# One transpose for two triangles of a query block's weights, with held constants, a halved last accumulator and a later half reload

## The chip, the cores and the metric

The kernel runs on one core of one Trainium2 chip. Its metric is the device time of one execution in microseconds (us). Three runs of the kernel before took 1166.5, 1167.22 and 1168.82 us; the median is 1167.22. One more execution was profiled; it took 1166.51 us, of which 1164.5 lie between its first and its last instruction (its span).

The engines are named as in the profile: PE multiplies matrices, PEld is its loading of weights, DVE, ACT and POOL work elementwise, SP issues the transfers (DMAs).

## What is computed

A trunk of two layers over 1024 tokens of width 1024, in float32: a gated linear attention layer (layer A), then a layer with dilated sliding-window attention (layer B), each closed by an output projection, a residual and a layer norm. The change touches above all the attention of layer B. Each of its 8 heads attends in three groups of windows, and the groups' results are weighted by a softmax over their log-sums:

```python
SWA_GROUPS = ((128, 1), (512, 4), (2048, 16))      # window, dilation
...
    kcat, vcat = with_prev(kb), with_prev(vb)      # the block before, then the block itself
    scores = jnp.einsum('brnqgpe,brnkge->brngpqk', qb, kcat)
    qi = jnp.arange(blk)[:, None]
    kj = jnp.arange(2 * blk)[None, :]
    rel = blk + qi - kj
    band = (rel >= 0) & (rel <= w_sub)
...
    p = jnp.exp(scores - m)
    den = jnp.sum(p, axis=-1)
    o = jnp.einsum('brngpqk,brnkge->brnqgpe', p, vcat) / jnp.moveaxis(den, -1, 3)[..., None]
```

In the first two groups `w_sub` is 128, a block's length. Query i of a block therefore sees key j of its own block where j <= i, and key j of the block before where j >= i. The two triangles share a 128x128 square but for the diagonal, which belongs to both.

## The kernel before

The program is not issued in the order in which it is written. Every instruction is recorded as an `Op`; `Sched.order` then walks through time with a table of costs, gives each instruction the engine that is free first (`S.vp`: DVE or POOL; `S.va`: DVE or ACT), and among those that could start at a time takes the one with the smallest `prio`, which is its place in the program plus a shift (`S.later`). The result is a fixed order on each engine. So a changed cost or one more instruction anywhere can change which instruction stands beside which elsewhere. Where PE waits for data of one stage, the order places matmuls of a projection (tile `acc`) between: they are the filler that keeps PE occupied.

Large matmuls use `float32r` operands split in a high and a low part (`split_hi` on ACT, `split_lo` on DVE or POOL), three matmuls for each product (`mm3`). Attention's own matmuls are float32, and the trace shows each as two records; a transpose (a matmul with `ident`) is one record.

The program's parts, in order:

- The start (in `layer_a`): x arrives transposed, in eight tiles `xf` of 128x1024 with weights `wf`, is split into `xh`, `xl`, and multiplied into eight accumulators `pro`. The first tile is loaded in two halves, the others whole. The small constants (`b2c`, `ident`, `ngc`, `lngc`, `lnbc`) are loaded among them.
- Layer A, head by head (gates, `levels`, `state_prep`, projections, `chunks`, `finish`), its results kept in DRAM as `ogA`. Within the last head `reload_og` brings the six tiles of heads 0 to 2 back (`ogf`) and splits them into `ogh`, `ogl`, the first half of the tokens and then the second.
- `out_ln` for both halves, then layer B: keys and values; for each unit u (a head) `q_proj`, `scores` and `attend`.
- `scores(u)` writes the weights P: for groups 1 and 0 in tiles of two query blocks, each block 128 or 256 keys wide (one block without a block before it, or two). DVE adds the mask and takes the maximum, ACT takes the exponential.
- `attend(u)`: P is scaled by `cw`; group 2 is transposed into `diag` and multiplied with V; then `turn` transposes the 128x128 pieces of P that groups 1 and 0 need, up to four into one PSUM tile `ms`, and ACT or DVE copies them to SBUF as `PT`. Group 1 takes 3 pieces for each of 4 residues, group 0 15 pieces in four calls. `pv` multiplies them with V into two banks `po`. In group 0 a piece of a block and the next block's piece for the same keys go through as one matmul 256 wide.
- `out_ln(1, ...)` for the first half of the tokens, and `out_ln_rows(j, ...)` for j = 4 to 7, the blocks of the second half: two accumulators of 512 columns, `bn_stats` of each, `bn_aggr`, ACT's two steps for 1/sqrt, two passes on DVE, and two stores. The last of these ends the program.

Of the kernel before, what the change touches and what calls it, by code (L numbers as in the profile page):

```python
# [134 lines left out]
class Op:  # L135
    __slots__ = ("engs", "calls", "reads", "writes", "prio", "deps", "nuse", "cost", "t0", "t1", "eng", "func",
                 "first", "succ", "left", "seq", "port")


class Sched:  # L140
# [4 lines left out]
    def __init__(self, tc, lat, pad):  # L145
# [5 lines left out]
        self.extra = 0.0  # L151
# [9 lines left out]
    def record(self, engs, meth, args, kw):  # L161
# [20 lines left out]
        if g is None:  # L182
            o = Op()
            o.engs, o.calls, o.reads, o.writes, o.cost = engs, [], [], [], [0.0] * len(engs)
            o.func, o.prio, o.seq = func, len(self.ops) + self.shift, len(self.ops)
            o.port = [shares_port(e, meth, outs, ins) for e in engs]
            self.ops.append(o)
        else:
            o = g
            if not o.calls:  # L190
                o.engs, o.cost, o.func = engs, [0.0] * len(engs), func
                o.port = [False] * len(engs)
                o.prio, o.seq = len(self.ops) + self.shift, len(self.ops)
                self.ops.append(o)
# [6 lines left out]
    def group(self):  # L201
        return _Group(self)

# [45 lines left out]
    def order(self):  # L249
# [62 lines left out]
        while n_done < len(ops):  # L312
            best = None
            for e in self.ENG:
                cand = None
                for o in ready[e]:
                    if o.t0 is not None:
                        continue
                    r = 0.0
# [24 lines left out]
            if o.func is not None and e == "ACT":  # L344
                new = act_set(o.func, cur_set)
                if new != cur_set:
                    c += 1.3
# [133 lines left out]

class _Landing:
# [93 lines left out]
def trunk(tc, xT, wP, wA, wA12, wAv3, w2, b2, ng, wO, wK, wV0, wV12, wB, wOB, lng, lnb,  # L576
          ident_d, lmask_d, cos_d, sin_d, bmask_d, rmask_d, lnr_d, out):
# [93 lines left out]
    ngc = const.tile([128, NK], F32, name="ngc")  # L671
    lngc = const.tile([128, 2, NK], F32, name="lngc")
    lnbc = const.tile([128, 2, NK], F32, name="lnbc")
# [5 lines left out]
    def load_consts():  # L679
        S.sync.dma_start(ident, ident_d)  # L680
        S.vector.memset(onesr.bitcast(F32), 1.0)
        S.sync.dma_start(ngc, ng)
        S.sync.dma_start(lngc, lng)
        S.sync.dma_start(lnbc, lnb)
# [18 lines left out]
    def layer_a(t2, t1, after):  # L703
        lmask = t2.tile([128, NLEV - 2, 32], U8, name="lmask")
        smask = t2.tile([128, 512], F32, name="smask")
        b2c = t2.tile([128, GH], F32, name="b2c")
# [59 lines left out]
        for kt in range(NK):  # L766
# [14 lines left out]
            for r in (hs(0), hs(1)) if kt == 0 else (slice(0, T),):  # L781
# [9 lines left out]
        S.sync.dma_start(lmf, lmask_d)  # L791
        S.vector.tensor_copy(lmask, lmf)
        S.sync.dma_start(b2c, b2)
        w2f = xtile(F32, "w2f", (96, 512))
        S.sync.dma_start(w2f, w2)
# [217 lines left out]
        for h in range(GH):  # L1013
# [3 lines left out]
            for f in ('qg', 'qVg', 'qg', 'vge')[h]:  # L1017
                {"g": lambda: proj_g(h), "q": lambda: proj_qk(h + 1), "V": proj_v12, "v": lambda: proj_v(3), "e": after}[f]()
            for g in range(2):
                chunks(h, g)  # L1020
                finish(h, g)

# [65 lines left out]
    def out_ln_rows(j, wo, gam, bet):  # L1088
        xr = [small("res", tag, 2) for tag in ("t1", "t2")]
        rt = []  # L1090
        st = hp.tile([128, 2, 6], F32, name="lnst", bufs=2)
        for f in range(2):
            fs = hs(f)
            with S.later(-EVAC):
                S.sync.dma_start(xr[f], x1t[j - 4][:, fs])
            acc = bank(1, 2 * j + f)
            for kt in range(NK):
                (oh, ol), (wh, wl) = ogs[kt], wo[kt]
                with S.group():
                    S.tensor.matmul(acc, blk(oh, j), wh[:, fs], start=(kt == 0), stop=False)  # L1100
                    S.tensor.matmul(acc, blk(oh, j), wl[:, fs], start=False, stop=False)
# [522 lines left out]
```

## Time and profile before

| what | us |
|---|---|
| median of three runs | 1167.22 |
| the profiled execution | 1166.51 |
| its span, first to last instruction | 1164.5 |
| PE busy | 1154.5 |
| DVE busy | 766.6 |
| ACT busy | 483.0 |
| POOL busy | 166.0 |

The granted clock of PE was 0.998 of full speed over the span. A row of the chain of waits gives a start, a length and the engine and tile whose work filled it ("x9" counts records); it follows from the last instruction back through whatever released each step. All instructions of the program's body carry the line of the one call that issues them (L441 before, L446 after), so groups are told apart by tiles.

### The profile page before, as it was taken

The page shows a single profiled execution, that of the slowest core. Times are in us where ns is not written, and L with a number is a line of the kernel's source. Part 1 is how long each engine was busy: PE and PEld are TensorE (multiplying, and loading weights), DVE is VectorE, ACT ScalarE, POOL GpSimd, SP SyncE. Part 2 cuts the span into 40 slices and gives each one's busy share as a digit, 9 for nine tenths or more (in the row PEclk, how much of TensorE's full clock was granted, in tenths as well). Part 3 has the DMA queues.
Part 4 walks back from the last instruction along what each step waited for, and adds up shares of the span by engine and source line. Part 5 has one row for each costly group of instructions (what it writes and reads, how often), then busy time and mean ns, then how long its engine had stood idle before and what let it go on. Part 6 is the DMA issues. An engine that isn't in the chain of part 4 may idle for free.

```text
span 1164.5 us, 19529 instructions
## 1 busy us (share of the span) xinstructions
PE 1154.5 (99%) x7748; PEld 980.5 (84%) x7748; DVE 766.6 (66%) x1494; ACT 483.0 (41%) x1020; POOL 166.0 (14%) x101
## 2 busy tenths in 40 slices
PE   9999999999999999999999999999999999999997
PEld 8888888889987888888888888888888888888885
DVE  6294952685967697764366657574757676646578
ACT  5355541555463345311214433435333543545242
POOL 1001000202222131311021202020202111103000
PEclk9999999999999999999999999999999999999999
DMA  7111122111143463543611111111142011034545
GB/s 259 64 39 37 66 81 90 39 56 55 56 169 127 145 216 128 188 138 115 193 55 38 37 38 56 38 55 38 38 164 38 20 38 34 24 93 145 183 142 181
DMA packets 93227, 108.18 MB, mean 93 GB/s; under 512 B 44016, under 2 KB 62064, under 8 KB 93136
## 3 DMA queue, kind: packets, MB, share of 16 engines
q1 hardware_dynamic: 93136, 106.94, 29.2%
q8 instruction: 61, 1.00, 0.4%
q14 instruction: 30, 0.25, 0.1%
HBM read 85.74 MB, written 21.17 MB: 92 GB/s over the span
## 4 chain that ended last, share of the span: by engine, by line
PE 98%; DVE 0%; DMA 0%; ACT 0%; SPq 0%; issue 0%; DVEq 0%; ACTq 0%
PE acc L441 65%; PE po L441 10%; PE lv L441 9%; PE vac L441 8%; PE ms L441 5%; PE pro L441 2%; DMA xf<-in_xT 0%; DVE rt L441 0%; SPq L441 0%; DVE diag L441 0%; ACT xh L441 0%; DVE lnst L441 0%; DVE ogl L441 0%; DVE oT L441 0%; DVEq L1617 0%
## 5 line engine op out<-in xcount | busy, mean ns | idle before, releaser
L441 PE MATMUL acc<-x1h,wh 128*128 128x512 f32 x608 | 250.5, 412 | 0.0
L441 PE MATMUL acc<-x1h,wl 128*128 128x512 f32 x608 | 237.5, 391 | 0.0
L441 PE MATMUL acc<-x1l,wh 128*128 128x512 f32 x608 | 237.0, 390 | 0.0
L441 ACT ACTIVATE wh<-wf 128x1024 fp32r<-128x1024 f32 (+2 forms) x105 | 108.5, 1034 | 289.2 <-PE acc L441 161.8
L441 POOL TENSOR_TENSOR wl<-wf,wh 128x1024 fp32r<-128x1024 f32 x41 | 98.1, 2392 | 693.3 <-ACT wh L441 517.6
L441 PEld LDWEIGHTS acc<-x1h,wl 128*128 128x128 f32 x608 | 114.1, 188 | 24.7
L441 PEld LDWEIGHTS acc<-x1l,wh 128*128 128x128 f32 x608 | 114.5, 188 | 21.3
L441 PEld LDWEIGHTS acc<-x1h,wh 128*128 128x128 f32 x608 | 114.4, 188 | 21.0
L441 DVE TENSOR_TENSOR wl<-wf,wh 128x1024 fp32r<-128x1024 f32 (+2 forms) x64 | 80.0, 1251 | 64.8 <-ACT wh L441 54.7
L441 ACT ACTIVATE P<-P,sts 128x128 f32<-128x128 f32 (+2 forms) x192 | 81.3, 425 | 63.0 <-DVE sts L441 62.5
L441 PE MATMUL acc<-xh,wh 128*128 128x512 f32 x256 | 102.3, 400 | 0.0
L441 PE MATMUL acc<-xh,wl 128*128 128x512 f32 x256 | 99.8, 390 | 0.0
L441 PE MATMUL acc<-xl,wh 128*128 128x512 f32 x256 | 99.8, 390 | 0.0
L441 DVE TENSOR_TENSOR t<-acc,cosT 128x512 f32<-128x512 f32 x60 | 41.4, 690 | 76.4 <-PE acc L441 76.3
L441 DVE TENSOR_TENSOR t<-acc,sinT 64x512 f32<-64x512 f32 x120 | 82.6, 688 | 1.6
L441 DVE CUSTOM_DVE_ANT_0 P<-lv,bmask 128x256 f32<-128x256 f32 (+1 forms) x128 | 46.8, 380 | 39.1 <-PE lv L441 38.5
L441 DVE TENSOR_TENSOR Q<-t,t 128x512 f32<-128x512 f32 x47 | 69.1, 1470 | 1.5
L441 PE MATMUL lv<-K,Q 128*64 128x64 f32 (+2 forms) x512 | 69.0, 286 | 0.0
L441 PEld LDWEIGHTS lv<-K,Q 128*128 128x128 f32 (+1 forms) x512 | 53.8, 163 | 9.7 <-issue 1.6
L441 PE MATMUL acc<-ogh,wh 128*128 128x512 f32 x152 | 60.2, 396 | 0.0
L441 PE MATMUL acc<-ogl,wh 128*128 128x512 f32 x152 | 59.4, 391 | 0.3 <-DVE ogl L441 0.2
L441 PE MATMUL acc<-ogh,wl 128*128 128x512 f32 x152 | 59.2, 390 | 0.0
(244 smaller groups left out, 2166.7 us busy)
## 6 DMA issues: line engine op xcount, KB each, us to landing
wf<-in_wB SPq DMA_DIRECT2D x32, 512.0 KB
wf<-in_wA SPq DMA_DIRECT2D x24, 512.0 KB
wf<-in_wO SPq DMA_DIRECT2D x16, 512.0 KB
wf<-in_wOB SPq DMA_DIRECT2D x16, 512.0 KB
wf<-in_wV SPq DMA_DIRECT2D x12, 512.0 KB
res<-in_xT SPq DMA_DIRECT2D x16, 256.0 KB
x1d<-rt SPq DMA_DIRECT2D x16, 256.0 KB
out<-rt SPq DMA_DIRECT2D x16, 256.0 KB
```

What stands on the lines that cost most here:

```text
L441: getattr(handle[o.eng], meth)(*[conv(a) for a in args], **{k: conv(v) for k, v in kw.items()})
```

## The change

- **Turning.** After the exponential of each pair of query blocks in groups 1 and 0, a masked copy on DVE (`above`: j > i) puts the upper triangle of the block before into the empty upper triangle of the own piece. `turn` now transposes four own pieces in a call (16 in a unit, with 8 in each group, in place of 27). From each transposed tile DVE takes `own` with a multiplication by the triangle `upto`, and `prev` with a masked copy (`below`) onto a tile that already holds the diagonal of the block before, made by DVE or POOL as a product with `ident`. Each `pv` of group 0 is now 128 wide.
- **Masks.** Two small loads and two casts for `above`, `below` and `upto`, at layer B's beginning.
- **Constants.** `b2`, `ng`, `lng`, `lnb` come as one tensor `par`; its load and those of `ident`, `lmf` and `w2f` are held until 20 us of the order's own time.
- **Start.** x tiles 1 and 2 are loaded and split in halves as tile 0 is; the high part of the first weights is made on DVE. The first table load of ACT counts nothing in the order's costs.
- **Last accumulator.** In `out_ln_rows(7)` the second 512 columns become two accumulators of 256; `bn_stats` takes 256 columns everywhere.
- **Reload.** The second half of `reload_og` follows the last head's first `chunks`, without its shift ahead.

```diff
             if kt < 2 or kt % 2 == 0:
...
-                split_hi(w[1][:, ks], w[0][:, ks])
+                if kt == 0:
+                    S.vector.tensor_copy(w[1][:, ks], w[0][:, ks])
+                else:
+                    split_hi(w[1][:, ks], w[0][:, ks])
...
-            for r in (hs(0), hs(1)) if kt == 0 else (slice(0, T),):
+            for r in (hs(0), hs(1)) if kt < 3 else (slice(0, T),):
...
             for g in range(2):
                 chunks(h, g)
                 finish(h, g)
+                if h == GH - 1 and g == 0:
+                    after(1)
...
+        for c0, n in ((0, 512), (512, 256), (768, 256)) if j == 7 else ((0, 512), (512, 512)):
+            acc = bank(1, 2 * j + (c0 + n) // 512)[:, :n]
...
+                S.vector.scalar_tensor_tensor(t[:, fs], xr[c0 // 512][:, fs], ALPHA, acc, op0=OP.mult, op1=OP.add)
+                for q in range(c0, c0 + n, 256):
+                    S.vector.bn_stats(out=st[:, q // 256, :], in_=t[:, q % 512:q % 512 + 256])
...
+                    if g < 2:
+                        prev, own = pieces(P, g, j0)
+                        S.vector.copy_predicated(own, above.to_broadcast(list(own.shape)), prev)
...
-                turn_blocks(t[:, :len(bl) * 128], bl)
+                with S.group():
+                    for i in range(4):
+                        p, o = P[g, j0 + i]
+                        S.tensor.transpose(pt[:, i, :], blk(p[:, o:], BL[g][j0 + i][2] // 128 - 1), ident)
+                for i in (0, 2):
+                    front = pieces(P, g, j0 + i)[0]
+                    n = front.shape[1]
+                    S.vp.tensor_mul(prev[:, i + 2 - n:i + 2], front, ident[:, None, :].to_broadcast([128, n, 128]))
+                S.vector.tensor_mul(own, pt, upto.to_broadcast([128, 4, 128]))
+                S.vector.copy_predicated(has(prev), below.to_broadcast(list(has(prev).shape)), has(pt))
+                return own, prev
...
+            for n0 in (0, 4):
+                own, prev = turn(0, n0)
+                for i in range(4):
+                    n = n0 + i
+                    out_n = po[n // 4][:, i * 128:i * 128 + 128]
+                    if n:
+                        pv(n // 4, out_n, blk(Vc[0], n - 1), prev[:, i, :])
+                    pv(n // 4, out_n, blk(Vc[0], n), own[:, i, :], last=(i == 3))
...
-    def reload_og():
-        with S.later(-EVAC):
-            for half in range(2):
-                for kt in range(6):
-                    load_og(ogA[kt], kt, p0, lambda: small("ogf", "a", 13), (half,))
+    def reload_og(half):
+        with S.later(0 if half else -EVAC):
+            for kt in range(6):
+                load_og(ogA[kt], kt, p0, lambda: small("ogf", "a", 13), (half,))
```

The order of instructions, at three places. First PE, in the attention of unit 0, from the product of `diag` (group 2) to the transposes of group 0; `ms` rows are transposes, `po<-PT` products with V, `lv` the next unit's scores, `acc` filler. Before:

```order
L441 MATMUL po<-diag,V_5473 128x128 x8
L441 MATMUL ms<-ident,P 128x128 x6
L441 MATMUL acc<-x1h_4300,wh 128x512
L441 MATMUL acc<-x1l_4314,wh 128x512
L441 MATMUL acc<-x1h_4300,wl 128x512
L441 MATMUL po<-PT,V_5393 128x128 x9
L441 MATMUL ms<-ident,P 128x128 x7
L441 MATMUL lv<-K_5166,Q 64x64 x16
L441 MATMUL po<-PT,V_5393 128x128 x3
L441 MATMUL po<-PT,V_4457 128x256 x2
L441 MATMUL ms<-ident,P 128x128 x8
```

And now:

```order
L446 MATMUL po<-diag,V_5481 128x128 x8
L446 MATMUL ms<-ident,P 128x128 x4
L446 MATMUL acc<-x1h_4302,wh 128x512
L446 MATMUL acc<-x1l_4316,wh 128x512
L446 MATMUL acc<-x1h_4302,wl 128x512
L446 MATMUL po<-PT,V_5401 128x128 x2
L446 MATMUL lv<-K_5174,Q 64x64 x16
L446 MATMUL po<-PT,V_5401 128x128 x10
L446 MATMUL ms<-ident,P 128x128 x8
L446 MATMUL lv<-K_5008,Q 128x128
```

Fewer transposes stand between; the second row of `po<-PT` (one `own`, one `prev`) stands where the nine products of group 1 stood, with the same three filler matmuls ahead of it.

Second DVE, at the same place; `t` and `Q` belong to the rotation of the next unit's queries, `og<-po` takes group 2's result. Before:

```order
L441 TENSOR_TENSOR t_6212<-acc,cosT 128x512
L441 TENSOR_TENSOR t_6222<-acc,sinT 64x512 x2
L441 TENSOR_TENSOR Q<-t_6212,t_6222 128x4x8x16
L441 COPY og<-po 128x64x4 x4
L441 COPY PT<-ms 128x512
L441 ISA P,sts<-lv,rmask 128x64
```

And now:

```order
L446 TENSOR_TENSOR t_6231<-acc,cosT 128x512
L446 TENSOR_TENSOR t_6242<-acc,sinT 64x512 x2
L446 TENSOR_TENSOR PT<-ms,upto 128x512
L446 TENSOR_TENSOR Q<-t_6231,t_6242 128x4x8x16
L446 COPY og<-po 128x64x4 x4
L446 COPY_PREDICATED PT<-below,ms 128x2x128
L446 TENSOR_TENSOR PT<-ms,upto 128x512
L446 COPY_PREDICATED PT<-below,ms 128x2x128
L446 TENSOR_TENSOR PT<-P,ident 128x128
L446 TENSOR_TENSOR PT<-P,ident 128x256
```

The first tile's multiplication stands ahead of `Q`, and its masked copy behind the four copies `og<-po`; four turning instructions stand where one copy stood, since ACT made the others.

Third ACT, in the last head of layer A, where the reloaded tiles (`ogf`) are split; `sq<-po` begins the normalization of that head's first half. Before:

```order
L441 ACTIVATE ogh_3556<-ogf 128x512
L425 ACT_TABLE_LOAD
L441 ACTIVATE sg<-sg 128x2048
L441 ACTIVATE ogh_3563<-ogf 128x512
L441 ACTIVATE ogh_3570<-ogf 128x512
L441 ACTIVATE ogh_3577<-ogf 128x512
L441 ACTIVATE ogh_3584<-ogf 128x512
L441 ACTIVATE sq<-po 128x512 x2
L441 ACTIVATE sq<-sq 128x512
```

And now:

```order
L430 ACT_TABLE_LOAD
L446 ACTIVATE sg<-sg 128x2048
L446 ACTIVATE ogh_3556<-ogf 128x512
L446 ACTIVATE ogh_3563<-ogf 128x512
L446 ACTIVATE sq<-po 128x512 x2
L446 ACTIVATE ogh_3570<-ogf 128x512
L446 ACTIVATE ogh_3577<-ogf 128x512
L446 ACTIVATE ogh_3584<-ogf 128x512
L446 ACTIVATE sq<-sq 128x512
```

Two of the second half's splits stand ahead of `sq<-po` behind the table load instead of four, and three stand behind it.

More of the change, by code (lines that the diff above doesn't have):

```diff
@@ L202, in group, with hold @@
         return _Group(self)
+    def hold(self, us):
+        return _Hold(self, us)
     def later(self, n):
@@ L318, in order @@
                         continue
-                    r = 0.0
+                    r = o.least
                     for d in o.deps:
@@ L679, in load_consts @@
     def load_consts():
-        S.sync.dma_start(ident, ident_d)
+        with S.hold(20.0):
+            S.sync.dma_start(ident, ident_d)
+            S.sync.dma_start(par, par_d)
         S.vector.memset(onesr.bitcast(F32), 1.0)
-        S.sync.dma_start(ngc, ng)
-        S.sync.dma_start(lngc, lng)
-        S.sync.dma_start(lnbc, lnb)
     def rsqrt_rows(dst, src_ps, scale, tmp):
@@ L1089, in out_ln_rows @@
         xr = [small("res", tag, 2) for tag in ("t1", "t2")]
-        rt = []
-        st = hp.tile([128, 2, 6], F32, name="lnst", bufs=2)
+        rt = [small("rt", "a", 13) for _ in range(2)]
+        st = hp.tile([128, 4, 6], F32, name="lnst", bufs=1)
         for f in range(2):
-            fs = hs(f)
             with S.later(-EVAC):
-                S.sync.dma_start(xr[f], x1t[j - 4][:, fs])
-            acc = bank(1, 2 * j + f)
+                S.sync.dma_start(xr[f], x1t[j - 4][:, hs(f)])
+        for c0, n in ((0, 512), (512, 256), (768, 256)) if j == 7 else ((0, 512), (512, 512)):
+            acc = bank(1, 2 * j + (c0 + n) // 512)[:, :n]
+            cs, fs = slice(c0, c0 + n), slice(c0 % 512, c0 % 512 + n)
             for kt in range(NK):
@@ L1149, in layer_b @@
         S.sync.dma_start(rmask, rmask_d)
+        above, below = (p1.tile([128, 1, 128], U8, name=n, bufs=1) for n in ("above", "below"))
+        upto = p1.tile([128, 1, 128], F32, name="upto", bufs=1)
+        tri = small("tri", "d", 4).rearrange("p (a b) -> p a b", a=4)
+        S.sync.dma_start(tri[:, 0:2], tri_d[:, 0:2])
+        S.sync.dma_start(upto, tri_d[:, 2:3])
+        S.vector.tensor_copy(above, tri[:, 0:1])
+        S.vector.tensor_copy(below, tri[:, 1:2])
         cosT = page(p0, F32, "cosT")
@@ L1279, in g_proj, with pieces @@
             project(wB[u, 3], xs, evac)
+        def pieces(P, g, j0):
+            p, o = P[g, j0 + 1]
+            n = 1 if g or not j0 else 2
+            v = p[:, o + 256 - n * 256:o + 256].rearrange("p (a two b) -> p a two b", a=n, two=2)
+            return v[:, :, 0], v[:, :, 1]
         def scores(u):
@@ L1368, in attend, with turn, has @@
             U[u]["og"] = og
-            def turn(blocks, g):
-                t = small("PT", "d", 4)
-                bl = []
-                for j, part in blocks:
-                    p, o = P[g, j]
-                    o += part * 128
-                    bl.append(p[:, o:o + 128])
-                turn_blocks(t[:, :len(bl) * 128], bl)
-                return t.rearrange("p (a b) -> p a b", a=4)
+            def turn(g, j0):
+                own, prev = (small("PT", "d", 4).rearrange("p (a b) -> p a b", a=4) for _ in range(2))
+                pt = ps.tile([128, 4, 128], F32, name="ms", bufs=2)
+                def has(x):
+                    return x.rearrange("p (a two) b -> p a two b", two=2)[:, :, 1] if g else x[:, 0 if j0 else 1:]
+                with S.group():
[9 more added lines that the diff above has]
+                return own, prev
             for g in (2, 1, 0):
@@ L1571, in _arrays @@
         "wOB": c(np.stack([cols(swo, e * 128) for e in range(8)])),
-        "lng": c(np.asarray(inputs["ln_g"]).reshape(2, 8, 128).transpose(2, 0, 1)),
-        "lnb": c(np.asarray(inputs["ln_b"]).reshape(2, 8, 128).transpose(2, 0, 1)),
+        "par": c(np.concatenate([np.asarray(inputs[n]).reshape(-1, 128).T
+                                 for n in ("ln_g", "ln_b", "gla_norm_g", "gla_b_a2")], axis=1)),
         "lnr": c(np.stack([np.broadcast_to(np.asarray(inputs[n])[1], (128, 1024)) for n in ("ln_g", "ln_b")])),
```

88 lines of the change are left out of this document (38 added, 50 removed).

## The prediction

> **What bounds the kernel now.** I read the page's busy times first, then its chain of waits, then what PE waited for.
>
> ```profile
> span 1164.5 us, 19529 instructions
> PE 1154.5 (99%) x7748; PEld 980.5 (84%) x7748; DVE 766.6 (66%) x1494; ACT 483.0 (41%) x1020; POOL 166.0 (14%) x101
> PE 98%; DVE 0%; DMA 0%; ACT 0%; SPq 0%; issue 0%; DVEq 0%; ACTq 0%
> ...
> PE pro L441 <- ACT xh L441: 0.7, 1, 0.7
> PE acc L441 <- DVE ogl L441: 0.2, 1, 0.2
> ```
>
> PE is busy for all but 10.0 us of the span, and the chain that ended last is PE for 98%. The two last rows are PE's waits beside one at the very start: 0.9 us. So almost nothing is to be had by ending waits; what is to be had is work taken off PE, the start, and the tail behind the last matmul. The attention of layer B fills this stretch (a row gives PE, PEld, DVE, ACT, POOL busy, clock, DMA):
>
> ```profile
> 610.00:1080.00 470.00, 469.95 (x2640) 401.28 (x2636) 304.97 (x837) 203.05 (x630) 70.90 (x43) 1.00 0.21 56
> ```
>
> PE is never without work there; DVE is busy 65%. Every matmul saved here is time saved, as long as the other engines deliver in time.
>
> **Turning, on PE.** The pieces of the chain in unit 0's attention, with the groups of all units behind them:
>
> ```profile
> 655.17 0.76 PE ms L441 x7
> ...
> 659.79 0.66 PE ms L441 x6
> ...
> 661.15 2.01 PE po L441 x18
> 663.15 0.77 PE ms L441 x7
> ...
> 666.73 0.87 PE ms L441 x8
> ...
> 668.52 1.74 PE po L441 x10
> 670.26 0.33 PE ms L441 x3
> ...
> L441 PE MATMUL ms<-ident,P 128*128 128x128 f32 x248 | 34.1, 273 | 0.1
> L441 PE MATMUL po<-PT,V 128*128 128x128 f32 x240 | 32.1, 276 | 0.0
> L441 PE MATMUL po<-PT,V 128*128 128x256 f32 x96 | 25.1, 381 | 0.0
> ```
>
> The means of a group (273 ns) hold the pipeline's latency; what a transpose costs the stream is its share of the chain. The five `ms` rows are 31 transposes in 3.39 us: 0.109 us each, and 31 x 8 units are the 248 of the group. The change has 16 in place of 27 for groups 1 and 0, so 11 x 8 = 88 go: **-9.6 us**.
>
> Against it stand the products. 18 records 128 wide take 2.01 us, 0.112 each, 0.223 a product. In the row of 1.74 us six records are 256 wide and four 128 wide, so a 256-wide record takes (1.74 - 4 x 0.112) / 6 = 0.216, and the product 0.431. A unit has six of these (96 records / 2 / 8); each becomes two products of 0.223, 0.016 us more: 48 x 0.016 = **+0.75 us**. PE's balance is -8.85 us.
>
> The Trainium skill would price this lower: its page "TensorE: Matmul & The Clock Gate", section "Back-to-back issue gap", gives about 81 ns for a matmul of 128 columns in a stream with weight loads. By that the transposes are worth 88 x 0.081 = 7.1 us, an estimate. The trace's 0.109 disagrees, and I keep it.
>
> **Turning, on DVE, POOL and ACT.** What is added there must be hidden behind PE.
>
> ```profile
> L441 DVE COPY_PREDICATED Dg<-lmask,lv 128x256 f32<-128x256 uint8 x24 | 10.7, 445 | 3.8 <-ACT AT L441 2.3 <-PE lv L441 1.2
> L441 DVE TENSOR_TENSOR t<-acc,cosT 128x512 f32<-128x512 f32 x60 | 41.4, 690 | 76.4 <-PE acc L441 76.3
> L441 DVE COPY PT<-ms 128x512 f32<-128x512 f32 x12 | 8.3, 692 | 27.4 <-ACT PT L441 13.4 <-PE ms L441 12.6 <-ACT P L441 1.4
> L441 DVE COPY PT<-ms 128x384 f32<-128x384 f32 x8 | 4.5, 558 | 5.2 <-PE ms L441 5.2
> ```
>
> DVE gets 64 masked copies into P (128 or 256 wide, at most 445 ns: 28.5 us), 32 multiplications of a turned tile (690 ns: 22.1), 32 masked copies out of it (between 445 and 692 ns: 14.2 to 22.1), and 28 of the 64 diagonal products, the rest being POOL's (at most 445 ns: 12.5). It loses 20 copies (12.8). At most +72 us in 470, so DVE goes from 65% to at most 80%. Its total isn't the bound; **when** each result comes is. The masked copies into P are out of the way: P then waits for `cw`, which comes over several transfers. The turned tiles are in the way: PE waits for `own` and `prev` directly. The tightest place is the second product of the first short `po<-PT` row, which needs the first `prev`. DVE at this place before:
>
> ```profile
> 655.91 1.39 DVE L441 TENSOR_TENSOR t<-acc,sinT 64x512 f32<-64x512 f32 x2
> 657.33 2.11 DVE L441 TENSOR_TENSOR Q<-t,t 128x512 f32<-128x512 f32 x1
> 659.29 1.39 DVE L441 COPY og<-po 128x256 f32<-128x256 f32 x4
> ...
> L441 DVE TENSOR_TENSOR Q<-t,t 128x512 f32<-128x512 f32 x47 | 69.1, 1470 | 1.5
> ```
>
> By the new order the multiplication (0.69) comes ahead of `Q`, and the masked copy (0.445) behind the four copies. If everything shifts, the copies end at 659.29 + 1.39 + 0.69 = 661.37 and `prev` is there at 661.8. PE reaches that product one `ms` record fewer ahead (eight and four transposes where seven and six stood), at 661.15 - 0.11 + 0.22 = 661.26. So PE waits up to 0.55 us. If `Q` takes its group's mean of 1.47 us (last row) instead of 2.11, all is 0.64 earlier and nothing is waited for. The later turns have more filler before their first use in the order. I take 0.2 us a unit, between none and 0.55 at one turn of each of 8 units: **+1.5 us**, bounds 0 and +4.4.
>
> ACT loses 44 copies and is nowhere near the bound. The two loads of masks are 192 KB at the head of layer B, ahead of all its projections, and their first use stands behind those of keys and values; DMA is at 0.21 in the window above. Nothing; late masks would hold only unit 0's copies.
>
> **Start.** PE finished tile 0 of x, then waited for tile 1:
>
> ```profile
> 5.31 0.63 ACT L441 ACTIVATE xh<-xf 128x512 fp32r<-128x512 f32 x1 [0.75 <-DMA xf<-in_xT]
> 8.22 1.06 ACT L441 ACTIVATE xh<-xf 128x1024 fp32r<-128x1024 f32 x1 [1.42 <-DMA xf<-in_xT]
> 9.34 0.40 PE L441 MATMUL pro<-wh,xh 128*128 128x272 f32 x1 [0.66 <-ACT xh L441]
> ```
>
> ACT starts when the whole tile has landed, 8.22. Half a tile lands earlier by up to half the tile's flow, and splits in 0.63 instead of 1.06, so even a half landing at 8.0 is ready by 8.65, when PE is done with tile 0 (9.34 - 0.66 = 8.68). The held constants were issued behind tile 2 and can only help. **-0.65 us**, between 0 and -0.66, since the first matmul waits as before for the first half tile. Splitting the first weights on DVE changes nothing that PE waits for; holding `ident` and `par` costs nothing, as their first users stand behind the first head's projections in the program.
>
> **Reload.** The reported wait of 0.2 us hides a larger loss:
>
> ```profile
> 352.35 0.48 PE L441 MATMUL acc<-ogh,wh 128*128 128x512 f32 x1
> ...
> 355.03 0.50 PE L441 MATMUL acc<-ogl,wh 128*128 128x512 f32 x1 [0.23 <-DVE ogl L441]
> ...
> 1151.38 5.45 PE acc L441 x24
> ```
>
> Seven matmuls start from the first of these rows up to the second, 2.68 us; by the third row 24 take 5.45, 0.227 each, so seven take 1.59: about 1.0 us is lost to the chain of `oT`, `ogh`, `ogl` of the last head. The change lets `sq<-po` go ahead of three of the reloaded splits on ACT (as long as the `xh` row of 128x512, 0.63 us each), so this chain starts earlier. **-0.7 us**, between 0 and -1.0: part of the chain waits for PE's own `lv` products just ahead, and stays.
>
> **Tail.** The rows behind the last matmul, and the nearest ones of half the width:
>
> ```profile
> 1156.86 0.69 DVE L441 SCALAR_TENSOR_TENSOR rt<-res,acc 128x512 f32<-128x512 f32 x1 [1.15 <-PE acc L441]
> 1157.58 0.69 DVE L441 BATCH_NORM_STATS2 lnst<-rt 128x6 f32<-128x512 f32 x1
> ...
> L441 DVE SCALAR_TENSOR_TENSOR S<-S,dec,ms 128x256 f32<-128x256 f32 x24 | 11.5, 478 | 10.9 <-PE ms L441 10.5
> ...
> 279.66 2.52 PE acc L441 x21
> ```
>
> Both DVE steps behind the last accumulator are halved. The first goes from 0.69 to 0.48; no 256-wide statistics were recorded, so I take the same 0.2 off (bounds 0 and half, 0.35). On PE 24 matmuls 512 wide (5.45 us) become 48 of 256; 21 of that width took 2.52, so 48 take 5.76: +0.3. Sum **-0.1 us**, between +0.1 and -0.25.
>
> **Sum.** -8.85 + 1.5 - 0.65 - 0.7 - 0.1 = -8.8 us. From the profiled execution's 1166.51 that is 1157.7; the median of the runs shown is 0.7 above that execution, which puts the median at 1158.4. With the rounding that the stalls deserve I say **1158 us**. With every bound at its good end it is 1167.2 - 8.85 - 0.66 - 1.0 - 0.25 = 1156.4, with the bad ones 1162.9.
>
> **Rivals.**
>
> *DVE becomes the bound of units 4 to 6.* In those units the gate projections come later in the program, so a unit has less filler of its own, and each of four turns takes DVE 1.1 to 1.4 us (0.69 and 0.445 to 0.69) with PE waiting for the result. For it: DVE's 80% is a mean, and it works in bursts. Against it: the 20 copies `PT` of before stood behind 33 us of idle time of DVE (their two rows), most of it a wait for ACT or PE, so DVE is there before its data. Price: 0.4 us more for each of four turns of the last four units, 6.4 us: near 1164.
>
> *Slower: POOL's diagonal products hold the turn up.* 36 of the 64 products are POOL's, in line behind its long subtractions, and DVE and POOL exclude each other:
>
> ```profile
> 357.57 2.41 POOL L441 TENSOR_TENSOR wl<-wf,wh 128x1024 fp32r<-128x1024 f32 x1
> ...
> 358.17 2.89 DVE L441 TENSOR_TENSOR wl<-wf,wh 128x1024 fp32r<-128x1024 f32 x1 [0.30 <-ACT wh L441]
> ...
> L441 DVE TENSOR_TENSOR wl<-wf,wh 128x1024 fp32r<-128x1024 f32 (+2 forms) x64 | 80.0, 1251 | 64.8 <-ACT wh L441 54.7
> ```
>
> POOL held from 357.57 to 359.98, and the DVE instruction beside it ended at 361.06, 1.08 us after that: it had waited. If each of 32 masked copies `prev` waits for a POOL product in line, PE waits at every turn. From 0.32 us a turn (10.3 us gained elsewhere / 32) the kernel is slower; at 0.6 us, a quarter of a 2.4 us subtraction, it is 1167.2 - 10.3 + 19.2 = 1176. Against it: a product needs only the scaled P, as the transpose does, and 6 us pass between the transposes at 655.17 and their products at 661.15. The Trainium skill's page "SBUF — State Buffer", section "Who interferes with whom", says the same of a DVE instruction with two inputs in SBUF beside a POOL instruction that reads SBUF: one fully blocks. The trace agrees, with the 2.89 us above against the group's mean of 1.25.
>
> *A transpose is worth less than its share.* If a quarter of the 0.109 us were the handing over between shapes, it would stay in the stream: +2.4 us, near 1160.6. For it: neighbours change with the order. Against it: the five `ms` rows give 0.109 to 0.110 whether three or eight stand together, so nothing of it is paid once a row. By the 81 ns of the Trainium skill's page "TensorE: Matmul & The Clock Gate" the time would come out near this too.
>
> *Not what it says: transposes were free.* If PE's order left them in gaps, the 9.6 us would not come, and the time would be 1167.2 plus 0.75 and 1.5 less 1.45, 1168. The chain carries every one of them, so this is hardly possible.
>
> **How the numbers follow.** The forecast, 1155 to 1160: 72%. A transpose worth less, 1160 to 1161: 4%. DVE the bound, 1161 to 1165: 15%. POOL in line, above 1169.5: 4%. Transposes free, or gains given back in part, 1165 to 1169.5: 3%. Below 1155, should the order's small shifts end losses that I didn't see: 2%. The range 1155 to 1163 holds the forecast and half of DVE's rival, some 83%. A measurement of this kernel tells about 0.2% (2.3 us) from no change; faster by more 93%, within it 3%, slower 4%.
>
> **What would show it.** 160 `ms<-ident,P` records and 0.109 us of chain for each; 432 `po<-PT` records, all 128 wide; PE busy near 1146. PE's waits on DVE tile `PT` show the stall: below 3 us in total by the forecast, above 5 by the first rival, on units 4 to 6; in the second rival DVE's `PT` waits for POOL. The wait for `xh` at the start gone, the seven matmuls after the last `lv` product in 1.6 to 2.0 us. Wrong would be a PE whose records thin out in 610 to 1070 without a named wait, or transposes whose neighbours grow.

## The result, and the profile after

The changed kernel took 1158.24 us in the median of five runs (1158.02 to 1159.76), beside 1168.25 for the kernel before: the ratio is 0.992, with a 95% interval of 0.9908 to 0.9932. The forecast was 1158. Its profiled execution took 1158.02 us; from the page:

```profile
span 1156.2 us, 19776 instructions
PE 1145.3 (99%) x7780; PEld 975.7 (84%) x7780; DVE 816.8 (71%) x1653; ACT 462.4 (40%) x970; POOL 187.1 (16%) x135
```

The span is 8.3 us shorter and PE is busy 9.2 us less; DVE has 50 us more work. What PE waited for (us in all, times, longest):

```profile
PE po L446 <- DVE diag L446: 0.9, 2, 0.6
PE po L446 <- DVE PT L446: 0.8, 1, 0.8
PE ms L446 <- ACT P L446: 0.2, 1, 0.2
```

The wait for `xh` at the start is gone, and there are four new waits in three rows, 1.9 us, all in attention. The chain of waits (start, length, work) is PE nearly throughout and so gives milestones:

```profile
5.11 24.68 PE pro L446 x192
...
350.25 5.46 PE acc L446 x24
...
652.94 0.87 PE ms L446 x8
...
657.66 0.44 PE ms L446 x4
658.10 0.70 PE acc L446 x3
658.80 0.44 PE po L446 x4
...
662.76 0.87 PE ms L446 x8
...
1145.74 2.89 PE lv L446 x24
```

The first row ends the start, at 29.79; `ms x8` at 652.94 begins unit 0's turning; the last row ends PE's work, at 1148.63. In the kernel before these are 30.80, 655.17 and 1156.83. So the 8.3 us part into four stretches:

| stretch | before | changed | difference |
|---|---|---|---|
| to the end of `pro` | 30.80 | 29.79 | -1.01 |
| from there to unit 0's turning (holds the reload) | 624.37 | 623.15 | -1.22 |
| from there to the last matmul | 501.66 | 495.69 | -5.97 |
| behind the last matmul | 7.67 | 7.57 | -0.10 |

0.31 of the third is the halved last accumulator's own cost: 48 matmuls of 256 columns take 5.76 us where 24 of 512 took 5.45. Attention itself thus gained 6.28 us, where the sum of PE's work said 8.85. **2.57 us are missing, and most of them are new stalls.** By the windows below PE stands 1.94 us of them. A wait takes somewhat more from the stream of matmuls than PE's idle time shows, as a record of 0.39 us lets the next one start after 0.227: by an estimate up to 0.16 us at each of the four waits. Some 0.3 us belong to no wait at all (e12, below). PE's work itself came out as worked out: 20 transposes in the three `ms` rows take 2.18 us, 0.109 each, and the groups of instructions hold the counts that were named.

```profile
L446 PE MATMUL ms<-ident,P 128*128 128x128 f32 x160 | 22.3, 273 | 0.2 <-ACT P L446 0.2
L446 PE MATMUL po<-PT,V 128*128 128x128 f32 x432 | 53.9, 276 | 0.8 <-DVE PT L446 0.8
```

The stalls aren't at the place that the prediction called the tightest. There, the second product of the first `po<-PT` row starts with its row at 658.80, without a wait. They are in the second half of attention. The windows show it (length, then PE, PEld, DVE, ACT, POOL busy, granted clock, DMA); first before, then changed:

```profile
850.00:1000.00 150.00, 150.00 (x859) 127.93 (x859) 105.10 (x303) 62.30 (x208) 25.93 (x16) 1.00 0.20 50
1000.00:1080.00 80.00, 79.95 (x454) 68.37 (x453) 46.02 (x126) 41.24 (x108) 10.52 (x9) 1.00 0.30 92
```

```profile
610.00:850.00 240.00, 240.00 (x1342) 206.44 (x1341) 177.59 (x471) 88.44 (x287) 49.48 (x41) 1.00 0.20 54
850.00:1000.00 150.00, 148.88 (x878) 125.69 (x877) 120.04 (x361) 59.62 (x211) 27.54 (x22) 1.00 0.17 41
1000.00:1072.00 72.00, 71.18 (x399) 61.69 (x398) 53.99 (x143) 31.53 (x76) 14.60 (x14) 1.00 0.31 96
```

Up to 850 PE never stands. From 850 to 1000 (units 4 and 5 and the beginning of 6) DVE is busy 80% of the time, 70% before, and PE stands 1.12 us; behind 1000 it stands 0.82 us. There, in unit 7, DVE and POOL meet:

```profile
1055.15 2.13 DVE L446 TENSOR_TENSOR PT<-P,ident 128x128 f32<-128x128 f32 x2 [0.28 <-PE po L446]
...
1053.19 5.22 POOL L446 TENSOR_TENSOR ogl<-ogf,ogh 128x512 fp32r<-128x512 f32 x4
```

DVE waited for PE to free a `PT` buffer (a product writes into the second of a turn's two; four buffers are two turns). Then its two products took 2.13 us beside POOL's subtractions, where their group's mean is 0.31 each, and PE waited 0.8.

### The profile page after: what moved, and what is told of

It reads as the page before. It is cut to its first block, busy times and chain, and to the rows that moved or that the text cites. A ratio compares the mean times of both kernels' runs of the same rounds, so it can differ in the third digit from the quotient of the medians.

```text
span 1156.2 us, 19776 instructions
## 1 busy us (share of the span) xinstructions
PE 1145.3 (99%) x7780; PEld 975.7 (84%) x7780; DVE 816.8 (71%) x1653; ACT 462.4 (40%) x970; POOL 187.1 (16%) x135
## 4 chain that ended last, share of the span: by engine, by line
PE 96%; DVE 2%; DMA 1%; ACT 0%; issue 0%; POOL 0%; DVEq 0%; SPq 0%; POOLq 0%; ACTq 0%
PE acc L446 64%; PE lv L446 9%; PE po L446 9%; PE vac L446 8%; PE ms L446 4%; PE pro L446 2%; DVE t L446 0%; DMA xf<-in_xT 0%; DVE PT L446 0%; DMA wf<-in_wB 0%; POOL wl L446 0%; DVE P L446 0%; DVE rt L446 0%; ACT P L446 0%; DVE zz L446 0%
## 5 line engine op out<-in xcount | busy, mean ns | idle before, releaser
L446 POOL TENSOR_TENSOR wl<-wf,wh 128x1024 fp32r<-128x1024 f32 x39 | 93.5, 2396 | 634.6 <-ACT wh L446 450.9
L446 DVE TENSOR_TENSOR wl<-wf,wh 128x1024 fp32r<-128x1024 f32 (+2 forms) x66 | 83.7, 1268 | 61.3 <-ACT wh L446 48.4
L446 DVE TENSOR_TENSOR Q<-t,t 128x512 f32<-128x512 f32 x45 | 62.2, 1383 | 1.3
```

The costliest lines, as they stand in the source:

```text
L446: getattr(handle[o.eng], meth)(*[conv(a) for a in args], **{k: conv(v) for k, v in kw.items()})
```

## The experiments

Twelve kernels were timed beside the kernel before, in four to eleven runs each. Its median on the chips used was 1167.26, 1168.11, 1167.54 and 1167.71, so ratios are compared, and 0.001 of ratio is 1.2 us; an interval is about 0.0013 to either side. The stretches are those of the table above, read from each kernel's chain.

| kernel | median us | ratio | to end of `pro` | to turning | to last matmul | behind |
|---|---|---|---|---|---|---|
| changed again (e13) | 1158.35 | 0.9920 | 30.26 | 623.09 | 495.66 | 7.59 |
| turning alone (e1) | 1160.44 | 0.9944 | 30.94 | 624.30 | 495.39 | 7.87 |
| turning undone (e2) | 1164.62 | 0.9977 | 29.88 | 623.17 | 502.77 | 7.08 |
| transposes twice (e3) | 1169.20 | 1.0020 | 30.07 | 623.59 | 507.49 | 7.35 |
| last accumulator whole (e4) | 1159.40 | 0.9930 | 30.55 | 623.27 | 495.48 | 8.20 |
| reload undone (e5) | 1159.98 | 0.9932 | 30.04 | 624.42 | 497.08 | 7.66 |
| halves undone (e6) | 1159.39 | 0.9927 | 30.88 | 623.19 | 495.71 | 7.32 |
| hold undone (e7) | 1158.62 | 0.9921 | 30.23 | 623.23 | 495.96 | 7.78 |
| products on POOL (e9) | 1157.79 | 0.9915 | 29.64 | 623.17 | 495.46 | 7.63 |
| `ogl` on DVE (e11) | 1158.28 | 0.9927 | 29.32 | 623.62 | 496.46 | 7.10 |
| `prev` in place (e12) | 1156.79 | 0.9907 | 30.17 | 623.17 | 493.45 | 7.31 |
| in place, on DVE (e14) | 1163.80 | 0.9962 | 30.38 | 623.34 | 501.14 | 7.14 |

All diffs below are against the changed kernel.

**The two halves of the change.** e1 undoes all but the turning: the edits of e4 to e7 below together, and

```diff
-                    c += 1.3 if cur_set else 0.0
+                    c += 1.3
```

e2 undoes the turning alone; the masks, `pieces` and the masked copies into P go, and `turn` and its calls are those of before:

```diff
-            def turn(g, j0):
+            def turn(blocks, g):
...
-            for r0 in (0, 2):
-                own, prev = turn(1, 2 * r0)
+            for r in range(4):
+                t = turn([(2 * r, 0), (2 * r + 1, 0), (2 * r + 1, 1)], 1)
```

> The kernel before with the turning alone (one transpose for two triangles, its masks, and the small constants in one tensor); start, reload and last accumulator as before. Theory: the terms add, and turning gives PE's 8.85 us less some 2.5 us of new stalls, about 6.3 us: near 1162 us beside 1168.2 for the kernel before; in its trace units 4 to 7 hold the stalls. Rival: turning is worth little because DVE's work eats it, and the gain comes from start and reload: 1165 us or more.

> The changed kernel with the turning of before; held constants, halves at the start, halved last accumulator and later reload stay. Theory: start 1.0 and reload 1.1 us gained, last accumulator 0.2 lost by the two traces: near 1166.3 us beside 1168.2 before. Rival of the run above: 1161 to 1163 us. PE should show none of the stalls of units 4 to 7.

The turning gives 6.8 us (1160.44 beside 1167.26), the rest 2.6 (1164.62), together 9.4 where the change as a whole gave 10.0 and 9.2 in two sets of runs. So they add within the spread of the runs, and the stalls belong to the turning: e1 shows the waits on `diag` and `PT` with the same 0.9 and 0.8 us, e2 shows neither. e1 was expected to gain 6.2 and e2 1.9; by the spans of their profiled executions, 1158.5 and 1162.9 beside 1164.5, they gained 6.0 and 1.6.

**The price of a transpose.** Each transpose of `turn` stands there twice, 128 more in all.

```diff
-                    for i in range(4):
+                    for i in (0, 1, 2, 3, 0, 1, 2, 3):
                         p, o = P[g, j0 + i]
                         S.tensor.transpose(pt[:, i, :], ...
```

> The changed kernel with each of the four transposes of a turn issued twice into the same place: 128 more transposes, the results the same. By the chain's price of 0.109 us they cost 14.0 us: near 1172 us beside 1158.2 for the changed kernel. By 81 ns each 10.4 us, near 1168.6. If a quarter of the price were the handing over between shapes, 10.5 us as well. Turned tiles come up to 0.44 us later at each turn, which the filler should cover; if it does not, above 1174.

PE is busy 1159.1 us, 13.8 more, 0.108 for each of the 128. Its chain prices them alike in long rows and short:

```profile
653.66 1.31 PE ms L446 x12
...
656.35 0.87 PE ms L446 x8
```

By the ratio the time rose by 11.7 us only, and by the profiles the stretch by 11.8. The time alone would not have told 0.109 us a transpose from the lower price in the expectation; PE's busy time and the rows do, and they rule the rival of a cheaper transpose out. Most of what is missing to 14.0 are waits that went: none on `diag` or `PT` is left, and PE stands 0.23 us in the stretch where it stood 1.95. Why they went isn't parted: PE has more work of its own between, and POOL took work from DVE too (202.0 us busy for 187.1, DVE 809.1 for 816.8).

**DVE and POOL together.** In layer B the subtractions `ogl` are taken from POOL.

```diff
-            split_lo(lo[:, hs(half)], f, hi[:, hs(half)])
+            (S.vector if dve else S.vp).tensor_sub(lo[:, hs(half)], f, hi[:, hs(half)].bitcast(F32))
...
-            load_og(ogB[kt], kt, p1, lambda: small("ogf", "a", 13))
+            load_og(ogB[kt], kt, p1, lambda: small("ogf", "a", 13), dve=True)
```

> The changed kernel with the low parts of the tiles reloaded for the last projection (ogl from ogf) made by DVE alone instead of DVE or POOL. In the changed kernel POOL makes four in a row in unit 7, and beside them two diagonal products on DVE take 2.13 us and PE loses about 1 us. Theory, POOL's instruction holds DVE's: the loss goes, near 1157.3 us beside 1158.2, and the products take 0.3 us each. Rival, the turn waits for a free buffer of the turned tiles or for DVE's own load: no gain, or up to 1 us slower by seven more subtractions of 0.69 us on DVE.

The two products now take 0.48 us where they took 2.13, and the wait on `PT` falls from 0.8 to 0.3. The Trainium skill's page "SBUF — State Buffer", section "Who interferes with whom", says that a DVE instruction with two inputs in SBUF contends with a POOL instruction that reads SBUF; the two durations agree with it. Yet the stretch did not shrink (496.46 beside 495.69): PE waits for `S` and `sum` besides, 0.2 each. The second isn't DVE's load. It stands in the last projection, behind a late transfer of its weights, and e5 has it too (below), whose order there is the changed kernel's. The instruction's delay beside POOL is shown; whether ending it is worth time is not.

**All products on POOL.** This is the prediction's slower rival, made into a kernel.

```diff
-                    S.vp.tensor_mul(prev[:, i + 2 - n:i + 2], front, ...
+                    S.gpsimd.tensor_mul(prev[:, i + 2 - n:i + 2], front, ...
```

> The changed kernel with all 64 diagonal products on POOL (28 of them were DVE's). It tests the prediction's slower rival. Rival: each masked copy waits for a product in POOL's line behind subtractions of 1.3 to 2.4 us, 0.3 us or more at each of 32 turns: 10 us or more slower than the changed kernel, 1168 or more, with PE waiting for PT in most units. Theory: the planner's order leaves each product some us of room, and only the units that are tight already (4, 5, 7) lose: 1 to 3 us, 1159 to 1161, PE's named waits in attention 3 to 5 us instead of 1.9.

Neither came: 1157.79, not slower than the changed kernel at all. The wait on `PT` is gone, the 0.9 us on `diag` stay; the stretch is 0.2 us shorter, so most of the 0.8 was lost again elsewhere. POOL has room; its products wait for a buffer, not PE for them:

```profile
L446 POOL TENSOR_TENSOR PT<-P,ident 128x128 f32<-128x128 f32 x40 | 22.3, 571 | 35.2 <-PE po L446 27.3 <-DVE og L446 4.0 <-ACT P L446 2.8
```

Of the 35.2 us that POOL stood before these products, 27.3 were for PE to release a `PT` buffer.

**No second buffer.** The diagonal product and the lower triangle go into P's own front block, whose upper triangle has been copied out by then.

```diff
-                own, prev = (small("PT", "d", 4).rearrange(...) for _ in range(2))
+                own = small("PT", "d", 4).rearrange(...)
+                prev = [blk(P[g, j0 + i][0][:, P[g, j0 + i][1]:], 0) for i in range(4)]
...
-                    S.vp.tensor_mul(prev[:, i + 2 - n:i + 2], front, ...
+                    S.vp.tensor_mul(front, front, ...
...
-                S.vector.copy_predicated(has(prev), below..., has(pt))
+                for i in (0, 2):
+                    front = pieces(P, g, j0 + i)[0]
+                    n = front.shape[1]
+                    S.vector.copy_predicated(front, below..., pt[:, i + 2 - n:i + 2])
```

> The changed kernel, but the diagonal product and the lower triangle are written into P's own front block instead of a second PT buffer, so a turn takes one PT buffer and not two, and no product waits for PE to free one. DVE has 32 to 64 instructions more (two masked copies a turn, some 6 us in all). Theory: the stalls behind the turned tiles come from the buffers, the PT wait of unit 7 (0.8) and part of the others go: 0.8 to 1.5 us faster than the changed kernel, 1156.7 to 1157.5. Rival: the stalls come from DVE's combining of the weights and its 76% of load; they stay or grow with the added instructions, P's buffers are held longer: 1158 to 1160.

1156.79: the median is 1.56 us below the changed kernel's on the same chip, the best time of the study, though the intervals of the two ratios overlap (0.9893 to 0.9921, 0.9907 to 0.9932). The trace leaves less doubt: the stretch is 493.45, 2.2 us shorter, while it was 495.69 and 495.66 in two profiles of the changed kernel. PE's waits shrink to one row, the one at the very start:

```profile
PE pro L446 <- DVE Dg L446: 1.2, 1, 1.2
```

With the halved accumulator's 0.31 the attention gains 501.66 + 0.31 - 493.45 = 8.52 us of the 8.85 that PE's work said; the other 0.33 is no wait. But two things had changed: no product waits for a buffer, and as the products could now start early, the planner gave POOL 51 of them instead of 36, and more of P's scaling. The windows of this kernel show DVE relieved by 11.2 us just where PE had stood:

```profile
850.00:1000.00 150.00, 150.00 (x894) 127.93 (x893) 108.86 (x344) 60.71 (x209) 49.37 (x61) 1.00 0.18 41
1000.00:1072.00 72.00, 72.00 (x401) 62.53 (x400) 50.39 (x132) 33.85 (x87) 14.86 (x14) 1.00 0.32 96
```

**Buffers, or DVE's work?** The same kernel with all 64 products on DVE; this diff is against e12.

```diff
-                    S.vp.tensor_mul(front, front, ...
+                    S.vector.tensor_mul(front, front, ...
```

> The kernel with the diagonal products in P's own block (e12_prev_in_place), with all 64 of them on DVE. It parts two readings of that run's gain: there DVE was also relieved, 51 of the products went to POOL and its busy time fell from 816.5 to 798.6 us. Theory: it was the buffers; with DVE as busy as in the changed kernel (815 to 825 us) the stretch from the start of unit 0's turning to the last matmul stays at 493.5 us within 0.7, no PE wait on diag or on a turned tile above 0.3 us, 1156.5 to 1157.5. Rival: it was DVE's load; the waits on diag in units 4 and 5 come back and the stretch is 495 us or more, 1158 or more.

The rival is right, by far more than its own numbers: 1163.8, with the buffers as free as in e12. What PE waited for, and the windows:

```profile
PE ms L446 <- DVE P L446: 2.5, 3, 0.8
...
PE po L446 <- DVE PT L446: 1.0, 1, 1.0
PE po L446 <- DVE P L446: 0.9, 1, 0.9
PE po L446 <- DVE diag L446: 0.8, 2, 0.5
```

```profile
850.00:1000.00 150.00, 149.25 (x889) 126.73 (x888) 116.12 (x368) 59.95 (x211) 30.30 (x22) 1.00 0.18 42
1000.00:1072.00 72.00, 67.63 (x377) 57.56 (x377) 55.14 (x145) 31.01 (x78) 13.47 (x10) 1.00 0.32 97
```

DVE is back at 116.12 and 55.14 us, the waits on `diag` are back, and unit 7 loses 4.37 us. Most of that is one piece of DVE's line, beside POOL:

```profile
1051.94 5.66 DVE L446 TENSOR_SCALAR P<-P,cw 128x128 f32<-128x128 f32 x8
...
1052.58 3.82 POOL L446 TENSOR_TENSOR ogl<-ogf,ogh 128x512 fp32r<-128x512 f32 x3
```

Eight scalings take 5.66 us, 0.71 each; e12 has five at 1040.48 in 1.33, 0.27 each, with POOL idle. They stand ahead of the copies `og`, of `own` and `prev` in DVE's order, and PE waits for all of it. So the free buffer alone isn't worth anything. It isn't DVE's busy time alone either: e11 has 55.09 us in the same last window and PE stands 0.34.

The scalings also begin late, whatever POOL does. They need `cw`, the combining weights, which come back by a transfer; first the changed kernel's unit 7, then e14's:

```profile
1040.80 1.00 SPq L446 DMA_DIRECT2D cw<-cwd  x2
```

```profile
1046.91 1.00 SPq L446 DMA_DIRECT2D cw<-cwd  x2
```

In e14 a `wl` and a `sg` stand amid DVE's steps for the weights of this unit, so this transfer starts 6 us later; in e12 it starts at 1034.2. In the units with `diag` waits the time behind `cw` is short as well. From DVE's copy of `cw` to the first product with `diag` it is 14.4 to 19.7 us in units 0 to 3 and 7 of the changed kernel, but 3.2 to 3.5 in units 4 to 6, of which 4 and 5 wait. e14 has 3.2 to 3.5 there as well, e12 4.7 and the kernel before 3.6 to 4.8, both without a wait. So what seems to decide is how early DVE finishes the weights in the units with little filler. That is read from these orders, and no run changes it alone; how much of e14's loss is load, how much the late `cw` and how much the scalings' place beside POOL stays open.

**The smaller parts.** Each undoes one of them. e4 makes the last accumulator whole again:

```diff
-        for c0, n in ((0, 512), (512, 256), (768, 256)) if j == 7 else ((0, 512), (512, 512)):
+        for c0, n in ((0, 512), (512, 512)):
```

e5 puts the reload's second half back to the first, with its shift:

```diff
-... "e": lambda: after(0)}[f]()
+... "e": lambda: [after(0), after(1)]}[f]()
...
-                if h == GH - 1 and g == 0:
-                    after(1)
...
-        with S.later(0 if half else -EVAC):
+        with S.later(-EVAC):
```

e6 loads tiles 1 and 2 of x whole, and e7 sets the three holds to nothing:

```diff
-                if kt == 0:
-                    S.vector.tensor_copy(w[1][:, ks], w[0][:, ks])
-                else:
-                    split_hi(w[1][:, ks], w[0][:, ks])
+                split_hi(w[1][:, ks], w[0][:, ks])
...
-            for r in (hs(0), hs(1)) if kt < 3 else (slice(0, T),):
+            for r in (hs(0), hs(1)) if kt == 0 else (slice(0, T),):
```

```diff
-        with S.hold(20.0):
+        with S.hold(0.0):
```

e13 is the changed kernel itself.

> The changed kernel with the last accumulator 512 wide again, statistics still by 256. Theory: PE is 0.31 us shorter (24 matmuls of 512 for 48 of 256), and what DVE does behind the last matmul is longer by about 0.26 for rt and 0.4 for a second row of statistics: 0.2 to 0.4 us slower at most, so no difference that can be told, 1158.2 to 1158.7. Rival: the halves cost more on PE than they give behind it, 1157.9 to 1158.1.

> The changed kernel with the reload of the kernel before (both halves ahead of the last head's two finishing groups, both at early rank). Theory: the reload gave what the two milestones show, 1.1 us, all of it at the change from layer A to layer B, since the stretch up to the end of the projections for x is the changed kernel's own: about 1159.3. The seven matmuls behind the last lv product then start over 2.6 us again, and the chain shows DVE oT, ACT ogh and DVE ogl there. Rival: the rest of the kernel is reordered so far by it that part of the 1.1 us comes back later: 1158.2 to 1158.6.

> The changed kernel with tiles 1 and 2 of x loaded and split whole and the first weights' high part on ACT again. Theory of the prediction: only the wait for xh of tile 1 comes back, 0.65 us: about 1158.9, with end of pro 0.65 later. Rival: the halves also ended the slow spacing of the first ten matmuls, since PE starts later and without a gap, and all of the 1.0 us that the start gained goes: about 1159.3.

> The changed kernel with the loads of the constants issued as early as the planner likes again (no hold of 20 us); PE's order is the changed kernel's own. Theory of the prediction: the constants stand behind the tiles that PE waits for, holding them is worth nothing: 1158.2 within 0.3, end of pro within 0.1 us. Rival: their transfers share the DMA engines with tiles 1 to 3 of x, and 0.3 us or more of the start's gain is theirs: 1158.6 or more, with xf landing later.

> The changed kernel itself, on the chip and beside the runs of the other two. 1158.2 within 0.5. In its profile the end of pro tells of the start: in the seven kernels profiled so far that load tiles 1 and 2 in halves it lay between 29.3 and 30.6, and the later it was, the more of the first matmuls were spaced 0.225 us instead of 0.127. Theory: that is scatter of single executions and not of kernels, so this end of pro is again in that range but not at 29.79. Rival: the same kernel starts the same way each time, 29.8 within 0.1.

*Reload (e5).* 1.4 us slower by the ratio. The stretch with the reload is 624.42, that of the kernel before (624.37), where the eleven with the new reload lie from 623.09 to 623.62: the reload is worth 0.8 to 1.3 us, 1.2 in the two profiles compared above. The seven matmuls behind the last `lv` product take 2.68 us again, as expected. Another 1.4 is lost behind unit 0's turning (497.08), but not to the reload: from there on e5 has the changed kernel's order on every engine, and up to the last product with V it takes as long, 410.5 us beside 410.4. It lost them in the last projection (waits for `wol` 0.4, `sum` 0.2), where the chain runs through a late transfer of weights:

```profile
1100.21 6.12 DMA wf<-in_wOB
```

This execution was the slowest of its five, 1160.97 beside a median of 1159.98. So it is scatter of one execution, and so is, as far as the trace tells, the same wait for `sum` in e11.

*Halves (e6) and hold (e7).* e6 is 0.8 us slower by the ratio, within the interval; its start ends at 30.88, with a wait for `xh` of 0.3 us, not 0.65. The hold is worth nothing that can be seen in the time: 0.9921, and the start ends at 30.23, amid those that have it. Its one profile has a wait of 0.7 us for `xh`, where those with the hold show 0.3 at most; whether that is the hold's stays open.

*The start's scatter (e13).* The second profile of the same kernel ends its start at 30.26, not at 29.79. Eleven profiles with tiles 1 and 2 in halves end it between 29.32 and 30.55, 30.03 in the mean; three with whole tiles at 30.80, 30.88 and 30.94, 30.87 in the mean. So the halves give 0.84 us in the mean, and the 1.01 of the first pair is partly chance.

*Last accumulator (e4).* 1159.40 is above the 1158.7 expected at most, but 0.9930 beside 0.9920 is no difference that the runs can tell. The chain's rows behind the last matmul, of this kernel and of the changed one:

```profile
1149.32 0.70 DVE rt L446
1150.02 0.02 issue
1150.04 0.76 DVE lnst L446 x2
...
1152.46 0.74 DVE rt L446
```

```profile
1148.65 0.43 DVE rt L446
1149.09 0.02 issue
1149.11 0.44 DVE lnst L446
...
1151.20 0.75 DVE rt L446
```

DVE ends 3.90 us behind the last matmul (at 1149.30) in the one and 3.32 (1148.63) in the other; before it was 3.79. Beside PE's 0.31 more, the halves give 0.16 us over before. The time from there to the span's end, when the stores have landed, varies by more than that.

## Why the prediction was right

The time was right, and the main mechanism with it. Three of its smaller terms were off, in ways that nearly cancel, and that 1158 was met within 0.3 us is in part luck: the change from the kernel before, forecast as 8.8 us, is 8.3 by the two spans, but 10.0 by the medians of the first set of runs and 9.2 by the second.

- **Turning, on PE: -8.85. Right.** The changed kernel and e3 both show 0.109 us a transpose, and with all waits gone (e12) the attention gained 8.52. By the 0.081 us of the Trainium skill's page "TensorE: Matmul & The Clock Gate", section "Back-to-back issue gap", the 128 transposes of e3 would take 10.4 us, an estimate; PE's busy time grew by 13.8.
- **Stalls: +1.5, in fact +2.57 (of which 0.33 is no wait), and elsewhere.** "I take 0.2 us a unit" at the first `prev` of each unit was the step that failed. That place had no wait in unit 0. The stalls are in units 4, 5 and 7: on `diag` (0.9), where the combining weights, P's scaling and `diag` follow each other on DVE and ACT, and on one pair of products (0.8). This is the mechanism of the first rival, "DVE becomes the bound of units 4 to 6", at about a third of its price and without its wait at every turn. Its weak point was said there: DVE's 80% is a mean. DVE's load itself stayed under its bound (351.6 us of 462 in attention, 76%, at most 80% forecast). The prediction looked for the tight place in unit 0's turning; the profile before had a tighter one, the 3.6 to 4.8 us from `cw` to `diag` in units 4 to 6.
- **POOL in line, the slower rival: refuted,** by e9. But the reason given against it was incomplete. "A product needs only the scaled P" leaves out the buffer that it writes: most of POOL's idle time before its products was for a free `PT`. No wait of PE on `PT` came of it where all products were POOL's (e9). It probably drove them to DVE, since without a buffer to wait for POOL has 51 of them and not 36 (e12); that is argued, not tested by itself.
- **Start: -0.65, in the mean -0.84.** The bound of -0.66 took the reported wait as all that the halves could end, and took for granted that the first matmuls run as in the profile at hand. They scatter by a us from one execution to the next.
- **Reload: -0.7, in fact -1.2, by another way than forecast.** "This chain starts earlier" is wrong, and its bound of -1.0 was tight: by the prediction's own rows 2.68 - 1.59 = 1.09 us were lost there. The rows from the last `lv` product to `ogl`, before and changed:

```profile
351.99 0.61 PE L441 MATMUL lv<-qe,S 128*128 128x128 f32 x4
...
354.28 0.69 DVE L441 TENSOR_TENSOR ogl<-oT,ogh 128x512 fp32r<-128x512 f32 x1 [0.58 <-ACT ogh L441]
```

```profile
349.65 0.60 PE L446 MATMUL lv<-qe,S 128*128 128x128 f32 x4
...
351.94 0.69 DVE L446 TENSOR_TENSOR ogl<-oT,ogh 128x512 fp32r<-128x512 f32 x1 [0.59 <-ACT ogh L446]
```

  From the start of the first to the end of the second it is 2.98 us in both. What changed is what PE does meanwhile. Before, three matmuls on reloaded tiles stood between this `lv` and the first that needs the last head's `ogh`; now nine do, six more at 0.227 us, 1.36 us of cover, and the seven matmuls take 1.68 us, as the sign said. "Part of the chain stays" was true of the chain and wrong of the wait.
- **Tail: -0.1. Right** up to DVE's last step, with -0.16. To the end of the span it is +0.21 in the two profiles (0.31 - 0.10), as the last store took longer in the one after.

In the two profiles the sum is off by +1.07 for the stalls, -0.36 for the start, -0.52 for the reload and +0.31 at the end: +0.5, that is -8.3 for -8.8. Of the signs that were named, PE's wait on `PT` below 3 us was too narrow: it would have passed over the larger wait, on `diag`.

## What to carry to other kernels

Where PE is the bound, price a removed instruction by its share of PE's own chain, and trust it; then look for the stalls that the work moved to other engines brings where the filler is thinnest and the chain ahead of PE's data shortest in time, not where the first consumer stands. When products are given to "DVE or POOL", ask what they must wait for: an output buffer that is still held can send them to the busier engine. Writing into a block that is dead already, with most products then on POOL (e12), got back 2.2 of the 2.57 us, and the same with all products on DVE (e14) lost 5.5. A chain that can't be shortened can still be covered, so count the independent matmuls that stand behind its start.

## What the hardware showed beyond that

PE ran the first matmuls at about half speed, up to a moment that varies between executions of one kernel. In e13 the spacing of the 272-wide records is 0.225 us until past 6.65 and 0.125 after that; in the changed kernel's first profile it is 0.125 from 5.66 on, in e9 from 4.80. The granted clock doesn't tell. It reads 1.00 (behind the bracket) in both windows here, e4's with four matmuls and then the changed kernel's with six:

```profile
6.00:6.50 0.50, 0.50 (x4) 1.00 0.98 297
```

```profile
6.00:6.50 0.50, 0.50 (x6) 1.00 1.05 349
```

PE's first matmul starts at 1.25 in all of them, so the change comes under 3.6 to over 5.5 us behind it. The Trainium skill's page "TensorE: Matmul & The Clock Gate", section "Part 1: The HAM clock gate (the "warmup" mystery)", says that PE runs at half rate until it has been busy for a window of about 3.4 us, and that the window runs freely, so that the point varies from run to run. These traces agree with it in kind; the point varies more than the 0.5 us to either side that the section gives. For this kernel it is one part of a scatter of 1.2 us at the start (29.32 to 30.55), as large as two of the parts of this change. The landing of tiles is another: e7 has the short spacing from 5.02 on and still ends its start at 30.23, since PE then waits 0.7 us for `xh`.
